# A bidirectional linear-attention scan: block-diagonal products as 64x64 quarters, state and operator products as column halves

## The chip, the cores and the metric

The kernel runs on one core of one Trainium2 chip. The metric is the device time of one execution in microseconds (us); three timed runs of the kernel before gave 1756.57, 1759.63 and 1762.25 us.

## The reference, cut to what matters

One layer of a hybrid backbone over 128 context and 2048 latent tokens, width 1024. One input projection feeds two groups of channels: 512 channels of gated short convolution, and 512 channels (8 heads of 64) of RWKV-7 mixing, which is the part that the change touches. It is run once in each direction of time, and the two outputs are added:

```python
def step(S, inp):
    r_t, w_t, k_t, v_t, kk_t, a_t = inp
    s_kk = jnp.einsum('bdhij,bdhj->bdhi', S, kk_t)
    S = (S * w_t[..., None, :] - s_kk[..., :, None] * (kk_t * a_t)[..., None, :]
         + v_t[..., :, None] * k_t[..., None, :])
    return S, jnp.einsum('bdhij,bdhj->bdhi', S, r_t)

s_final, ys = lax.scan(step, s0.astype(f32), xs)      # d = 2 directions, h = 8 heads, S is 64 x 64
ys = jnp.moveaxis(ys, 0, 2)
y = ys[:, 0] + jnp.flip(ys[:, 1], axis=1)
```

The latent scans start from cached states, the context scans from zero; then come a group norm, a bonus term, gates, and one output projection with a residual and a final norm. All inputs and outputs are float32.

## The kernel before, in words

The program has three parts on one time axis. `phase1` (to about 1000 us) makes the projections and writes the scan's operands to DRAM. `phase2` is the scan (about 1000 to 1590 us), and `phase3` the output projection, which overlaps its end.

The scan works on chunks of 64 tokens. A *unit* is one chunk of one pair of heads in one direction. A *stage* holds 16 units: eight of direction 0 (group 0) and eight of direction 1 (group 1) of the same head pair, walking towards each other; there are 17 stages (16 of latent tokens, one of context). In each stage:

- `partL` loads the operands of the chunks into `rr`: five 64-column blocks for each unit on 128 partitions, the two heads of the pair one above the other (head 0 on partitions 0 to 63, head 1 on 64 to 127).
- `partM` makes products inside a chunk. `product` multiplies one operand with two others for each unit: F (one half-step of four units at a time, `F(0)` and `F(1)`) and G, which goes to `GA`. Since the two heads must not mix, `make_bd` first copies the left operand into a 128x128 block-diagonal tile `bd` (two copies on ACT for each of two operands and each group, line 779 is the copy helper), and each unit is one 128x128 product with half of it zero. DVE masks each four units out of PSUM (lines 893). `transposes` makes Q, `blocks` sends diagonal blocks of G to DRAM.
- `partI` inverts small triangular blocks on GpSimd (lines 926 to 934), `partU` and `partW` put them together (`psU`, `psW`: 32x32 products; `zb` is the result, again block-diagonal for two heads).
- `partB` multiplies `zb` with F (`psX`, one 128x128 product for each unit), copies the result on ACT into the stacked operands `stl` and `str`, and makes from these the operator E of each unit and head (`psE`, 128x128, lines 1029 and 1030).
- `partS` is the recurrence: for eight units in turn, in both groups, `psS` = E times the stacked state and values `sv` (two heads, each 128x128 by 128x64, line 1054); DVE scales the first 64 rows into the next unit's `sv` (line 1067); the other 64 rows are the output, which `finish` takes on (`psT` is its transpose).

Stages are pipelined: while the recurrence of stage s runs, `partB` and `partU` of stage s+1 and `partM` of stage s+3 (`LA = 3`) are emitted between its steps. `MORD` says which pieces of `partM` form one emitted step, and `ORDER` between which steps the other parts go. What the engines then see is an order that the framework's scheduler makes from this with a timeline of its own, so an instruction may move ahead of or behind others. PSUM is held in small pools: two buffers for `psF`, `psG`, `psQ` (`O.pm`), two for `psX`, `psE`, `psU`, `psW`, `psT` (`O.p2`), four for `psS`.

Of the kernel before, what the change touches and what calls it, by code (L numbers as in the profile page):

```python
# [681 lines left out]
MORD = ("Ff", "GgD", "", "Q")  # L682
# [8 lines left out]
def phase2(K):  # L691
# [8 lines left out]
    def setup_first():  # L700
# [20 lines left out]
        B.bd = ring(O.r1, 2, [128, 8, 128], "bd", zero)  # L721
        B.rr = ring(O.r1, 2, [128, 5, 8, 64], "rr", presetR)
# [12 lines left out]
    def setup_rest():  # L735
# [21 lines left out]
        B.zb = O.l1.tile([128, 2, 8, 128], F32, name="zb")  # L757
# [113 lines left out]
    def partM(s, st):  # L871

        at = S["at"][s]
        for gi, g in enumerate(st.g):
            d = g.d
            rr = g.rr
# [5 lines left out]
            def transposes():  # L882
                pq = O.pm.tile([128, 4, 128], F32, tag="m", name=f"psQ{s}_{gi}")
                for k in range(4):
                    T.transpose(pq[:, k, :], rr[:, 4, 2 * k:2 * k + 2, :].rearrange("p u t -> p (u t)"), B.idt[:])
                copy("q", g.Q, pq[:])

            def product(h, dst, w, x, mask, nm):
                ps = O.pm.tile([128, 4, 128], F32, tag="m", name=f"ps{nm}{s}_{gi}_{h}")
                for i in range(4):  # L890
                    u = h * 4 + i
                    T.matmul(ps[:, i, :].rearrange("p (a b) -> p a b", b=64), w[:, u, :], x[:, :, u, :], start=True, stop=True)  # L892
                V.tensor_tensor(dst[:, h * 4:h * 4 + 4, :], ps[:], mask.unsqueeze(1).broadcast_to((128, 4, 128)), ALU.mult)  # L893

            def blocks():
# [5 lines left out]
            F = lambda h: product(h, g.F, pb, rr[:, 2:4], B.msk[:, MF[d]], "F")  # L901
            GA = lambda h: product(h, g.GA, qb, rr[:, 1::-1], B.mkg[:, MG[d]], "G")
            ops = dict(Q=transposes, F=lambda: F(0), f=lambda: F(1), G=lambda: GA(0), g=lambda: GA(1), D=blocks)
            for piece in MORD:
                for c in piece:
                    ops[c]()
                yield
# [47 lines left out]
    def partW(s, st):  # L955
# [5 lines left out]
        for n in range(2):  # L961
            for g in st.g:
# [18 lines left out]
    def partU(s, st):  # L981
# [7 lines left out]
        rows = [(slice(sl * 64, sl * 64 + 32), slice(sl * 64 + 32, sl * 64 + 64)) for sl in range(2)]  # L989
        for u in range(16):  # L990
            for r0, r1 in rows:
                T.matmul(pu[r1, u, :], st.g[u // 8].GA[r0, u % 8, 96:128], st.zr[r0, u, :], start=True, stop=True)
        for r0, r1 in rows:
# [3 lines left out]
        for u in range(16):  # L997
            for r0, r1 in rows:
                T.matmul(pw[r0, u, :], B.bu[r1, u, :], st.zc[r1, u, :], start=True, stop=True)
        zf = B.zb[:].rearrange("p d u c -> p (d u) c")  # L1000
        for r0, r1 in rows:
# [9 lines left out]
    def partB(s, st):  # L1011
        for n in range(2):
            for gi, g in enumerate(st.g):
                us = half(g, n)
                g.E.append(tl([128, 4, 2, 128], "E", 4))
                px = O.p2.tile([128, 4, 128], F32, tag="s", name=f"psX{s}_{gi}_{n}")
                for i in range(4):
                    T.matmul(px[:, i, :], B.zb[:, gi, us.start + i, :], g.F[:, us.start + i, :], start=True, stop=True)  # L1018
# [395 lines left out]
```

## Time and profile before

| | |
|---|---|
| timed runs, median (lowest, highest) | 1759.63 us (1756.57, 1762.25) |
| profiled execution, first to last instruction | 1752.9 us |
| mean granted TensorE clock | 0.972 |
| busy TensorE / weight loads / VectorE / ScalarE / GpSimd | 1647.9 / 1558.8 / 1093.0 / 870.1 / 582.1 us |
| DMA | 335.69 MB, mean 192 GB/s |

The profiled execution has no time of its own beside its span; the timed runs lie 6.7 us above it. PE is TensorE's matmuls, PEld its weight loads, DVE VectorE, ACT ScalarE, POOL GpSimd, SP the DMA-issuing SyncE. A group line gives: line of the kernel, engine, operation, tiles written <- read, shapes, count | busy us, mean ns of one | idle time of the engine just before, and what ended it. For matmuls, `128*128` is the part of the array that is used, rows by columns. Spans of matmuls overlap, so the mean ns of one is not what one costs; that is read from start to start in the order of time. Rows of stretches give for each engine the busy us and, in brackets, the number of instructions, then the granted TensorE clock (PEclk), the share of time that DMA engines were busy, and GB/s.

### The profile page before, as it was taken

The page shows a single profiled execution, that of the slowest core. Times are in us where ns is not written, and L with a number is a line of the kernel's source. Part 1 is how long each engine was busy: PE and PEld are TensorE (multiplying, and loading weights), DVE is VectorE, ACT ScalarE, POOL GpSimd, SP SyncE. Part 2 cuts the span into 40 slices and gives each one's busy share as a digit, 9 for nine tenths or more (in the row PEclk, how much of TensorE's full clock was granted, in tenths as well). Part 3 has the DMA queues.
Part 4 walks back from the last instruction along what each step waited for, and adds up shares of the span by engine and source line. Part 5 has one row for each costly group of instructions (what it writes and reads, how often), then busy time and mean ns, then how long its engine had stood idle before and what let it go on. Part 6 is the DMA issues. An engine that isn't in the chain of part 4 may idle for free. (4 is left out here: it accounts for less than half of the span.)

```text
span 1752.9 us, 33041 instructions
## 1 busy us (share of the span) xinstructions
PE 1647.9 (94%) x12400; PEld 1558.8 (89%) x12400; DVE 1093.0 (62%) x2092; ACT 870.1 (50%) x1719; POOL 582.1 (33%) x1089
## 2 busy tenths in 40 slices
PE   5999899998999999999998989999999999899998
PEld 2889898998999998999998979899999999787886
DVE  5875788866567766567764544475776666656333
ACT  4534455534143433334442367687788787633222
POOL 0011111111011101011120587777777778223221
PEclk9899999999999999999999998899999999999999
DMA  9797778785557646477666585587677875746442
GB/s 367 208 234 220 233 241 246 232 255 151 148 160 227 169 147 174 135 258 217 195 214 225 173 196 135 141 192 187 174 198 189 191 185 120 180 151 206 151 144 90
DMA packets 315825, 335.69 MB, mean 192 GB/s; under 512 B 166985, under 2 KB 263881, under 8 KB 301585
## 3 DMA queue, kind: packets, MB, share of 16 engines
q1 hardware_dynamic: 243360, 324.52, 62.6%
q10 hardware_dynamic: 70944, 4.60, 2.9%
q0 software_dynamic: 1360, 4.46, 0.7%
q8 instruction: 98, 1.61, 0.4%
q14 instruction: 63, 0.51, 0.1%
HBM read 221.42 MB, written 112.08 MB: 190 GB/s over the span
## 5 line engine op out<-in xcount | busy, mean ns | idle before, releaser
L934 POOL TENSOR_TENSOR zt<-zt,ztmp 128x30 f32<-128x30 f32 (+7 forms) x510 | 197.3, 387 | 39.3
L1054 PE MATMUL psS<-sv,E 128*128 128x64 f32 x1088 | 155.1, 277 | 1.0 <-DVE sv L1067 0.6
L1029 PE MATMUL psE<-str,stl 128*128 128x128 f32 x1088 | 144.1, 281 | 11.3 <-DVE E L1030 7.0
L1054 PEld LDWEIGHTS psS<-sv,E 128*128 128x128 f32 x1088 | 145.4, 200 | 3.3 <-DVE sv L1067 0.8
L1029 PEld LDWEIGHTS psE<-str,stl 128*128 128x128 f32 x1088 | 131.8, 194 | 14.1 <-DVE E L1030 7.9
L931 POOL TENSOR_TENSOR ztmp<-ab,zt 128x60 f32<-128x60 f32 (+7 forms) x255 | 130.8, 513 | 19.2
L1067 DVE TENSOR_TENSOR sv<-psS,pc 64x128 f32<-64x128 f32 x254 | 69.2, 277 | 92.9 <-PE psS L1054 92.2
L779 ACT COPY bd<-rr 64x512 f32<-64x512 f32 x136 | 84.0, 617 | 75.7 <-DMA rr<-scr_ops 23.3
L323 POOL TENSOR_TENSOR shk<-rawl 128x384 f32<-128x384 f32 (+1 forms) x24 | 20.7, 861 | 291.9 <-ACT rawl L319 291.9
L1030 DVE TENSOR_TENSOR E<-psE,msk 128x512 f32<-128x512 f32 x136 | 92.7, 684 | 33.0 <-PE psE L1029 32.3
L892 PE MATMUL psF<-rr,bd 128*128 128x128 f32 x544 | 80.0, 295 | 16.2 <-ACT Q L779 9.8
L892 PEld LDWEIGHTS psF<-rr,bd 128*128 128x128 f32 x544 | 70.7, 203 | 20.4 <-ACT Q L779 12.9
L1350 POOL TENSOR_TENSOR z<-z,x 128x512 f32<-128x512 f32 x32 | 43.6, 1364 | 126.6 <-DVE z L1346 105.9
L1018 PE MATMUL psX<-F,zb 128*128 128x128 f32 x544 | 78.2, 297 | 3.2 <-ACT zb L777 2.3
L197 POOL TENSOR_TENSOR hslb<-kd,hshb 128x384 fp32r<-128x384 f32 (+1 forms) x24 | 26.7, 1113 | 164.0 <-ACT hshb L196 143.5
L160 PE MATMUL mmc<-h,w 128*128 128x384 f32 (+1 forms) x192 | 67.9, 354 | 13.4 <-ACT q1r L321 9.8
L323 POOL TENSOR_TENSOR shv<-rawl 128x384 f32<-128x384 f32 (+1 forms) x24 | 25.4, 1060 | 153.4 <-ACT rawl L319 153.4
L892 PE MATMUL psG<-rr,bd 128*128 128x128 f32 x544 | 72.0, 280 | 4.4 <-DVE F L893 4.4
L1018 PEld LDWEIGHTS psX<-F,zb 128*128 128x128 f32 x544 | 71.6, 209 | 4.0 <-POOL zt L934 1.9
L892 PEld LDWEIGHTS psG<-rr,bd 128*128 128x128 f32 x544 | 65.7, 193 | 5.0 <-DVE F L893 4.8
L161 PE MATMUL mmc<-h,w 128*128 128x384 f32 (+1 forms) x192 | 66.1, 344 | 0.0
L162 PE MATMUL mmc<-h,w 128*128 128x384 f32 (+1 forms) x192 | 65.7, 342 | 0.0
(307 smaller groups left out, 5205.4 us busy)
## 6 DMA issues: line engine op xcount, KB each, us to landing
w<-scr_wsp SPq DMA_DIRECT2D x68, 1024.0 KB, 7.3
scr_wsp<-w SPq DMA_DIRECT2D x34, 1024.0 KB, 6.0
rr<-scr_ops SPq DMA_DIRECT2D x64, 512.0 KB, 4.6
scr_ops<-sp SPq DMA_DIRECT2D x160, 192.0 KB, 5.2
wr<-in_win SPq DMA_DIRECT2D x34, 512.0 KB, 6.3
ab<-scr_at SPq DMA_DIRECT2D x34, 256.0 KB, 4.2
x<-in_x SPq DMA_DIRECT2D x17, 512.0 KB, 3.8
wadas<-in_wada SPq DMA_DIRECT2D x8, 1024.0 KB, 13.0
```

Of the source, the lines that this page charges most:

```text
L160: T.matmul(ps[:, :n], w[:, 0, k], hh[:, 0, k, :n], start=k == 0, stop=False)
L161: T.matmul(ps[:, :n], w[:, 0, k], hh[:, 1, k, :n], start=False, stop=False)
L162: T.matmul(ps[:, :n], w[:, 1, k], hh[:, 0, k, :n], start=False, stop=k == 7)
L779: (V.tensor_copy if k in ON_DVE else P.copy)(dst, src)
L892: T.matmul(ps[:, i, :].rearrange("p (a b) -> p a b", b=64), w[:, u, :], x[:, :, u, :], start=True, stop=True)
L931: G.tensor_tensor(tv, ab[:, j:j + 2, j + 2:32].unsqueeze(1).broadcast_to((128, kn, 2, n)), zt[:, :kn, j:j + 2].unsqueeze(3).broadcast_to(( ...
L934: G.tensor_tensor(zt[:, :kn, j + 2:32], zt[:, :kn, j + 2:32], tv[:, :, r], ALU.subtract)
L1018: T.matmul(px[:, i, :], B.zb[:, gi, us.start + i, :], g.F[:, us.start + i, :], start=True, stop=True)
L1029: T.matmul(pe[:, i, hd, :].rearrange("p (b t) -> p b t", b=2), g.lt[:, :, hd, us.start + k + i].rearrange("p b t -> p (b t)"), g.rt[:, :, ...
L1030: V.tensor_tensor(g.E[n][:, k:k + 2].rearrange("p a b c -> p (a b) c"), pe[:].rearrange("p a b c -> p (a b) c"), B.msk[:, ME[g.d]].unsquee ...
L1054: T.matmul(sp[gi][:, q, hd, :], g.E[n][:, k, hd, :], sv[:, u, hd, :], start=True, stop=True)
L1067: r = V.tensor_tensor(dst, sp[gi][0:64, q], B.pc[0:64, d, 2 * p:2 * p + 2, c:c + 1].broadcast_to((64, 2, 64)), ALU.mult)
```

## The change

The block-diagonal operands go. F, G and X are made as 64x64 quarters of the array: one for each head, with the other head's zero block left out, and the two groups put a head's result into different halves of the partitions (`place`), so that head 0 and 1 of group 0 and of group 1 use the four quadrants. `product` and `psX` now loop over both groups inside the unit loop and hold a PSUM buffer for each group. `zb` shrinks to 64 columns. E and S are made as two column halves: each 128x128 product becomes two with 128 rows and 64 columns of the array. `rr` gets a third buffer, `bd` goes. `MORD` and the number of `partM` steps between the recurrence's steps follow.

```diff
-MORD = ("Ff", "GgD", "", "Q")
+MORD = ("F", "f", "G", "gD", "Q", "q")
...
-        B.bd = ring(O.r1, 2, [128, 8, 128], "bd", zero)
-        B.rr = ring(O.r1, 2, [128, 5, 8, 64], "rr", presetR)
+        B.rr = ring(O.r1, 3, [128, 5, 8, 64], "rr", presetR)
...
-        B.zb = O.l1.tile([128, 2, 8, 128], F32, name="zb")
+        B.zb = O.l1.tile([128, 2, 8, 64], F32, name="zb")
...
-    def make_bd(t_, src):
-        copy("b", t_[0:64, :, 64:128], src[0:64])
-        copy("c", t_[64:128, :, 0:64], src[64:128])
+    def place(g, hd):
+
+        return 1 - hd if g.d == 0 else hd
+
+    def rows(i):
+        return slice(i * 64, i * 64 + 64)
...
-            pb, qb = B.bd(), B.bd()
-            make_bd(pb, rr[:, 0])
-            make_bd(qb, rr[:, 4])
...
-            def product(h, dst, w, x, mask, nm):
-                ps = O.pm.tile([128, 4, 128], F32, tag="m", name=f"ps{nm}{s}_{gi}_{h}")
-                for i in range(4):
-                    u = h * 4 + i
-                    T.matmul(ps[:, i, :].rearrange("p (a b) -> p a b", b=64), w[:, u, :], x[:, :, u, :], start=True, stop=True)
-                V.tensor_tensor(dst[:, h * 4:h * 4 + 4, :], ps[:], mask.unsqueeze(1).broadcast_to((128, 4, 128)), ALU.mult)
+        def product(h, w, xs, dst, mask, nm):
+            ps = [O.pm.tile([128, 4, 128], F32, tag="m", name=f"ps{nm}{s}_{gi}_{h}") for gi in range(2)]
+            for i in range(4):
+                u = h * 4 + i
+                for g, p_ in zip(st.g, ps):
+                    for hd in range(2):
+                        r = rows(hd)
+                        T.matmul(p_[rows(place(g, hd)), i, :].rearrange("p (a b) -> p a b", b=64), g.rr[r, w, u, :], g.rr[r, xs, u, :], start=True, stop=True)
+            for g, p_ in zip(st.g, ps):
+                V.tensor_tensor(dst(g)[:, h * 4:h * 4 + 4, :], p_[:], mask(g).unsqueeze(1).broadcast_to((128, 4, 128)), ALU.mult)
...
-                    r = slice(64 - i * 64, 128 - i * 64)
-                    copy("g", g.gs[64:128, 1, i, us], g.GA[r, us, 0:64])
+                    copy("g", g.gs[64:128, 1, i, us], g.GA[rows(place(g, i)), us, 0:64])
...
-            for r in (r0, r1):
-                copy("z", zf[r, :, r], st.zc[r])
-            copy("n", zf[r0, :, r1], pw[r0], True)
+            for i, r in enumerate((r0, r1)):
+                copy("z", zf[r, :, i * 32:i * 32 + 32], st.zc[r])
+            copy("n", zf[r0, :, 32:64], pw[r0], True)
...
+            px = [O.p2.tile([128, 4, 128], F32, tag="s", name=f"psX{s}_{gi}_{n}") for gi in range(2)]
+            for i in range(4):
+                for gi, g in enumerate(st.g):
+                    u = half(g, n).start + i
+                    for hd in range(2):
+                        r = rows(place(g, hd))
+                        T.matmul(px[gi][rows(1 - hd), i, :], B.zb[r, gi, u, :], g.F[r, u, :], start=True, stop=True)
...
-                px = O.p2.tile([128, 4, 128], F32, tag="s", name=f"psX{s}_{gi}_{n}")
-                for i in range(4):
-                    T.matmul(px[:, i, :], B.zb[:, gi, us.start + i, :], g.F[:, us.start + i, :], start=True, stop=True)
...
-                            T.matmul(pe[:, i, hd, :].rearrange("p (b t) -> p b t", b=2), g.lt[:, :, hd, us.start + k + i].rearrange("p b t -> p (b t)"), g.rt[:, :, hd, us.start + k + i], start=True, stop=True)
+                            for b, c in enumerate((H0, H1)):
+                                T.matmul(pe[c, i, hd, :].rearrange("p (b t) -> p b t", b=2), g.lt[:, b, hd, us.start + k + i], g.rt[:, :, hd, us.start + k + i], start=True, stop=True)
...
-                    T.matmul(sp[gi][:, q, hd, :], g.E[n][:, k, hd, :], sv[:, u, hd, :], start=True, stop=True)
+                    for m_ in (H0, H1):
+                        T.matmul(sp[gi][m_, q, hd, :], g.E[n][:, k, hd, m_], sv[:, u, hd, :], start=True, stop=True)
...
-                for _ in range((2, 2, 2, 1, 1, 0, 0, 0)[i]):
+                for _ in range((1, 1, 1, 1, 1, 1, 0, 0)[i]):
```

Where the scheduler then puts the instructions of TensorE is shown in the prediction, at the places of which it speaks. Of a name such as `psE_1_01` there, the first digit is the group and the next the half-step (of E, also the half of the half-step); the letter is the product, and the number after `x` counts equal products in a row.

More of the change, by code (lines that the diff above doesn't have):

```diff
@@ new lines, in F, with GA, transposes @@
+        def F(h):
+            product(h, 0, slice(2, 4), lambda g: g.F, lambda g: B.msk[:, MF[g.d]], "F")
+        def GA(h):
+            product(h, 4, slice(1, None, -1), lambda g: g.GA, lambda g: B.mkg[:, MG[g.d]], "G")
+        def transposes(gi):
+            g = st.g[gi]
+            pq = O.pm.tile([128, 4, 128], F32, tag="m", name=f"psQ{s}_{gi}")
+            for k in range(4):
+                T.transpose(pq[:, k, :], g.rr[:, 4, 2 * k:2 * k + 2, :].rearrange("p u t -> p (u t)"), B.idt[:])
+            copy("q", g.Q, pq[:])
@@ L896, in blocks @@
+        def blocks():
+            for gi, g in enumerate(st.g):
                 dg = tl([128, 8, 32], "dg", 1, O.rI)
@@ L899, in blocks @@
                 nc.scalar.dma_start(at[gi * 8:gi * 8 + 8].rearrange("u s b j i -> (s b j) u i"), dg[:])
[L901 to L907, printed above, removed]
+        ops = dict(Q=lambda: transposes(0), q=lambda: transposes(1), F=lambda: F(0), f=lambda: F(1), G=lambda: GA(0), g=lambda: GA(1), D=blocks)
+        for piece in MORD:
+            for c in piece:
+                ops[c]()
+            yield
     def partI(s, st):
@@ L1015, in partB @@
                 g.E.append(tl([128, 4, 2, 128], "E", 4))
[L1016 to L1018 removed]
                 for hd in range(2):
[L1020 removed]
+                    copy("x" if hd else "y", g.fs[64:128, :, hd, us], px[gi][rows(1 - hd)].rearrange("p u (b t) -> p b u t", b=2), True)
             yield
```

20 lines of the change are left out of this document (6 added, 14 removed).

## The prediction

> **What bounds the kernel now.** I read the page first (its busy times and its groups), then the stretches of the scan, then the order of time on TensorE inside one stage, and last the waits. The page's first part and the groups that the change touches:
>
> ```profile
> PE 1647.9 (94%) x12400; PEld 1558.8 (89%) x12400; DVE 1093.0 (62%) x2092; ACT 870.1 (50%) x1719; POOL 582.1 (33%) x1089
> ...
> L1054 PE MATMUL psS<-sv,E 128*128 128x64 f32 x1088 | 155.1, 277 | 1.0 <-DVE sv L1067 0.6
> L1029 PE MATMUL psE<-str,stl 128*128 128x128 f32 x1088 | 144.1, 281 | 11.3 <-DVE E L1030 7.0
> ...
> L1067 DVE TENSOR_TENSOR sv<-psS,pc 64x128 f32<-64x128 f32 x254 | 69.2, 277 | 92.9 <-PE psS L1054 92.2
> L779 ACT COPY bd<-rr 64x512 f32<-64x512 f32 x136 | 84.0, 617 | 75.7 <-DMA rr<-scr_ops 23.3
> ...
> L1030 DVE TENSOR_TENSOR E<-psE,msk 128x512 f32<-128x512 f32 x136 | 92.7, 684 | 33.0 <-PE psE L1029 32.3
> L892 PE MATMUL psF<-rr,bd 128*128 128x128 f32 x544 | 80.0, 295 | 16.2 <-ACT Q L779 9.8
> ...
> L1018 PE MATMUL psX<-F,zb 128*128 128x128 f32 x544 | 78.2, 297 | 3.2 <-ACT zb L777 2.3
> ...
> L892 PE MATMUL psG<-rr,bd 128*128 128x128 f32 x544 | 72.0, 280 | 4.4 <-DVE F L893 4.4
> ```
>
> TensorE is busy 94% of the span. Each float32 product of the program stands in the trace as two passes (544 state products, x1088), each with a weight load of its own, and 128*128 is the part of the array, rows by columns, that a pass uses. A busy share alone does not say that an engine is the bound, so next the scan, first its fifteen stages from the first to the last and then seven steady ones:
>
> ```profile
> core 0: us, PE busy (x) PEld busy (x) DVE busy (x) ACT busy (x) POOL busy (x), PEclk, DMA share, GB/s
> 1021.30:1493.90 472.60, 453.13 (x5354) 440.24 (x5354) 287.00 (x589) 368.98 (x706) 361.27 (x815) 0.96 0.71 172
> 1256.50:1469.20 212.70, 206.43 (x2537) 201.25 (x2536) 142.53 (x291) 172.31 (x332) 162.07 (x361) 1.00 0.77 185
> ```
>
> A steady stage takes 212.7 / 7 = 30.4 us, of which PE is busy 29.5, ACT 24.6, POOL 23.2 and DVE 20.4. PE waits under 1 us of a stage, and what it waits for there is short:
>
> ```profile
> PE psF L892 <- ACT Q L779: 3.7, 11, 0.8
> PE psE L1029 <- ACT stl L777: 1.1, 1, 1.1
> PE psE L1029 <- DVE E L1030: 1.0, 1, 1.0
> ```
>
> So the scan is bound by how fast TensorE takes passes, and the recurrence through the state is covered: sv on DVE waited 92.2 us for psS, and psS only 0.6 us for sv. The next limits are ACT and POOL, 6 to 7 us lower. That makes the price of a pass the whole question.
>
> **The price of a pass, of a small pass and of a switch.** The order of time on TensorE, at two places of a stage:
>
> ```profile
> 1240.87 0.56 PE L1054 MATMUL psS<-sv,E 128*128 128x64 f32 x4
> 1241.26 1.11 PE L1018 MATMUL psX<-F,zb 128*128 128x128 f32 x8
> 1242.21 0.33 PE L1054 MATMUL psS<-sv,E 128*128 128x64 f32 x2
> ...
> 1253.37 1.20 PE L992 MATMUL psU<-zr,GA 32*32 32x32 f32 x64
> 1254.50 1.10 PE L1054 MATMUL psS<-sv,E 128*128 128x64 f32 x8
> 1255.44 1.11 PE L892 MATMUL psF<-rr,bd 128*128 128x128 f32 x8
> 1256.48 0.24 PE L999 MATMUL psW<-zc,bu 32*32 32x32 f32 x2
> 1256.66 0.66 PE L1054 MATMUL psS<-sv,E 128*128 128x64 f32 x4
> 1257.24 1.19 PE L999 MATMUL psW<-zc,bu 32*32 32x32 f32 x62
> 1258.37 0.66 PE L1132 MATMUL psT<-idt,y 128*128 128x128 f32 x4
> ```
>
> From start to start, four S passes and eight X passes take 1242.21 - 1240.87 = 1.34 us, 0.112 us each, although S streams 64 columns and X 128: the 128-column weight load sets the S pass. The 64 passes of U, which use two different 32*32 squares in turn, take 1.13 us with the change of shape behind them, 0.018 each, so two squares work at once. What a change of shape costs: eight F passes should take 0.90 and psW starts 1.04 later, 0.14 over; four S passes between two pieces of psW take 0.58 in place of 0.45, 0.13 over; I take 0.15. U less 0.15 is 0.98 us for 32 rounds of two, 0.031 a round. Column strips of the array are seen at the start of the kernel:
>
> ```profile
> 34.33 1.06 PE L190 MATMUL psrow<-wadas,scp 128*32 128x512 f32 x8
> 34.33 0.16 PEld L190 LDWEIGHTS psrow<-wadas,scp 128*32 128x32 f32 x8 [0.24 <-issue]
> ```
>
> Eight passes, four times as wide as an X pass, on four strips: one after another they would be about 8 x 4 x 0.112 = 3.6 us, and they take 1.06, their eight weight loads 0.16. Strips load and work at the same time, each with its own moving data.
>
> **The state products S** become two 128*64 halves, both of which can load and stream together. A round then costs what a load and a stream of 64 columns cost; no row shows it, and I put it on the line between 0.031 (32 wide) and 0.112 (128 wide): 0.058. 1088 x 0.112 = 122 us becomes 1088 rounds x 0.058 = 63: **-58 us** (ends: 0, if halves loaded in turn, which psrow speaks against; -88 at U's round).
>
> **The operator products E** are 128 wide, so a round of two halves still streams as long as one pass did: 0 (0.112 against 0.112).
>
> **F, G and X** lose their zero blocks: 1632 passes, 183 us, become 3264 quarter passes. They cost half if four quarters run together, and nothing is won if two do. The source alternates both groups, so that four stand side by side; the schedule does not keep that. TensorE in a steady stage of before, from psE_0_01 to the next E pair (the first digit of a psS or psE is the group, and xN counts products):
>
> ```order
> L1029 MATMUL psE_1_01_14274<-str_10041,stl_10035 128x128 x4
> L1054 MATMUL psS_1_0_14436<-sv_13965,E_14248 128x64 x2
> L885 MATMUL psQ_0_14482<-idt_9262,rr_9282 128x128 x4
> L1018 MATMUL psX_0_1_14379<-F_9272,zb 128x128 x4
> L1054 MATMUL psS_0_0_14432<-sv_13956,E_14240 128x64 x2
> L1018 MATMUL psX_1_1_14387<-F_9275,zb 128x128 x4
> L1054 MATMUL psS_1_0_14436<-sv_13965,E_14248 128x64 x2
> L892 MATMUL psF_1_0_14503<-rr_9283,bd_9278 128x128 x4
> ```
>
> The same place of the program now:
>
> ```order
> L1041 MATMUL psE_1_01_14884<-str_10087,stl_10081 64x128 x8
> L1067 MATMUL psS_0_0_15078<-sv_14474,E_14848 64x64 x4
> L1067 MATMUL psS_1_0_15084<-sv_14483,E_14851 64x64
> L1026 MATMUL psX_0_1_15000<-F_9266,zb 64x128 x8
> L1067 MATMUL psS_1_0_15084<-sv_14483,E_14851 64x64 x3
> L887 MATMUL psF_0_1_15124<-rr_9278 64x128 x2
> L1026 MATMUL psX_1_1_15001<-F_9269,zb 64x128 x8
> L1067 MATMUL psS_0_0_15078<-sv_14474,E_14848 64x64 x4
> L1067 MATMUL psS_1_0_15084<-sv_14483,E_14851 64x64 x4
> L1041 MATMUL psE_0_10_15024<-str_10086,stl_10080 64x128 x8
> L887 MATMUL psF_1_1_15125<-rr_9279 64x128 x8
> ```
>
> The eight X quarters of one group stand together, then those of the other; so do both halves of F and the second of G. A group alone has two quadrants, so eight quarters are four rounds of two passes, 0.9 us, as four full products were. Only psG of the first half and psX of the first half alternate:
>
> ```order
> L887 MATMUL psG_0_0_15159<-rr_9278 64x128 x2
> L887 MATMUL psG_1_0_15160<-rr_9279 64x128 x2
> L887 MATMUL psG_0_0_15159<-rr_9278 64x128 x2
> L887 MATMUL psG_1_0_15160<-rr_9279 64x128 x2
> L887 MATMUL psG_0_0_15159<-rr_9278 64x128 x2
> L1041 MATMUL psE_1_11_15054<-str_10087,stl_10081 64x128 x8
> L887 MATMUL psG_1_0_15160<-rr_9279 64x128 x2
> ```
>
> Two half-steps in six cost half: 183 x 2/6 / 2 = **-30 us** (ends: -91 if TensorE reaches past eight waiting quarters to the other group's, 0 if never four).
>
> **Switches of shape.** Before, S, E, F, G, X and the transposes all used the whole array; now S and E use 128*64, F, G and X 64*64, Q and T all of it. Counted over the whole order, neighbours of different shape rise from 131 to 506, in a steady stage from 6 to about 27. 375 x 0.15 = **+56 us**. 303 of the 506 lie between 64*64 and 128*64, a pair that this trace does not show; if that pair were free, the term would be +11.
> The Trainium skill, "TensorEngine Tiling (Array Packing)", Key Properties, says that changing the tiling mode, not just the tile, drains TensorE; by it the term stays at +56, the sum at -32, and without it the sum would be -77. The trace agrees for the pairs it has (0.13 to 0.17 us).
>
> **The rest.** The 136 copies that make the block-diagonal operand leave ACT (84 us, 4.6 of its 24.6 in a stage), and two 617 ns steps between the load of rr and F. ACT is not the bound; PE's idle before psF, 16.2 us in all, is the most that could go. Against it I set new waits of DVE's 684 ns evictions, since both groups now take both buffers of the psF pool: 0 in the sum, 15 either way. What hid S's round trip (S, then DVE's sv, 277 ns) were 0.9 to 2 us of other passes between two S pairs; 0.9 to 1.8 us remain. DMA issues do not change but for a third rr buffer.
>
> **Sum.** -58 - 30 + 56 + 0 = -32 us against the profiled span of 1752.9: 1721. The timed runs have a median of 1759.63, 6.7 us over that span, which the change does not touch: **1728 us**. A steady stage would go from 30.4 to about 28.4.
>
> **The rivals.**
> *Switches between halves and quarters are free, or the queue reaches the other group's quarters:* 45 us less, or up to 60. Nothing in the trace shows it; the squares of U overtaking one another speak a little for the second. About 1683. Chance 0.16.
>
> *The clock.* The granted clock halves after a thin stretch and stays low; TensorE's order of time there, and the stretches:
>
> ```profile
> 1217.59 1.20 PE L992 MATMUL psU<-zr,GA 32*32 32x32 f32 x64
> 1218.72 1.10 PE L1054 MATMUL psS<-sv,E 128*128 128x64 f32 x8
> 1221.28 1.01 PE L892 MATMUL psF<-rr,bd 128*128 128x128 f32 x3 [1.46 <-ACT Q L779]
> ```
>
> ```profile
> 1214.40:1217.80 3.40, 3.40 (x42) 3.28 (x42) 1.86 (x5) 2.82 (x6) 2.93 (x7) 1.00 0.72 204
> 1217.80:1221.25 3.45, 2.02 (x72) 1.84 (x64) 1.25 (x4) 3.31 (x8) 2.90 (x8) 1.00 0.87 189
> 1221.25:1224.65 3.40, 3.37 (x16) 3.08 (x16) 0.00 (x0) 2.34 (x4) 2.28 (x7) 0.50 0.44 110
> 1224.65:1228.10 3.45, 3.45 (x71) 3.27 (x71) 0.39 (x2) 1.19 (x4) 0.00 (x0) 0.50 0.83 228
> 1228.10:1231.50 3.40, 3.40 (x17) 3.40 (x17) 3.17 (x5) 1.02 (x3) 2.69 (x5) 0.50 0.41 100
> ```
>
> In the second row of stretches PE works 2.02 of 3.45 us, about half of it on 32*32 squares, waits 1.46 for Q, and then runs at 0.50 for 10.25 us: 5.1 us lost. Quarters alone fill half the array and each switch is a gap, so the stretch U, S, G, W of every stage comes near that row, and a stretch of 64*64 passes may not bring the clock back. At one such loss in each of 17 stages, 87 us; the scan now loses (1 - 0.96) x 472.6 = 19: 1728 + 68 = 1796, slower. It decides from about seven losses more than now, (32 + 5.3) / 5.1. Against it: U and W lie behind S and G as before, and the wait for Q should go, since other passes now stand between Q and F. Chance 0.24.
> The Trainium skill, "TensorE: Matmul & The Clock Gate", HAM oscillation, tells of the same halving by windows of about 3.4 us; the rows agree.
>
> *Quarters of one group wait for each other*, because both write one PSUM buffer: a group alone then costs twice, an alternating pair what it did: 183 x (4/6 x 2 + 2/6) = 305 us in place of 153: 1880. U's two squares write one buffer and overlap. Chance 0.03.
> The Trainium skill, "TensorEngine Tiling (Array Packing)", Gotcha 1, forbids different row tiles the same bank at the same time; U's 0.018 us a pass disagrees.
>
> *PE's gain turns into waits* for DVE, ACT and the operator chain, 2 us a stage: about 1757, no change. PE waits under 1 us a stage now, but its order is fixed and the fill between S pairs is shorter. Chance 0.14.
>
> **How the numbers follow.** 0.43 for the forecast, 1728, with 15 us of waits either way. The range goes from the free switches (1683) to the clock (1796); outside lie 0.03 above and tails of both rivals, near 0.15. 0.3%, 5.3 us, is about what a measurement can tell from no change. Faster: 0.43 + 0.16 + 0.02 of the waits = 0.61; same 0.09; slower 0.24 + 0.03 + 0.03 = 0.30.
>
> **What would show it.** After: psS passes x2176 at about 0.03 us each from start to start; a psE piece of four products still 0.9 us; a psX piece of one group (eight quarters) 0.9 us, an alternating one 0.45; 0.15 us over at each change of shape; steady stages of 28 to 29 us at clock 1.00 and no more losses of clock than now. Steady stages under 26 us would say that switches are free; a mean clock under 0.93 in the scan, that the gate took it; PE idle of 2 us a stage, the waits.

## The result, and the profile after

The kernel after the change took 1838.52 us (median; 1837.4 to 1840.77) against 1760.94 us of the kernel before on the same chip: 1.0435 times as long, 95% interval 1.0411 to 1.0459. 1728 us were forecast, with a range of 1683 to 1796: the sign was wrong, and the time lies outside. The profiled execution spans 1837.3 us. Its page, TensorE's busy time and the groups that answer to those of before:

```profile
PE 1634.4 (89%) x16208; PEld 1488.4 (81%) x16208; DVE 1087.9 (59%) x2093; ACT 776.9 (42%) x1583; POOL 585.7 (32%) x1087
...
L1041 PE MATMUL psE<-str,stl 128*64 128x128 f32 x2176 | 169.8, 309 | 43.2 <-ACT stl L776 25.4
...
L887 PE MATMUL psF<-rr 64*64 64x128 f32 x1088 | 89.3, 312 | 60.1 <-DMA rr<-scr_ops 18.6
...
L1067 PE MATMUL psS<-sv,E 128*64 128x64 f32 x2176 | 112.6, 233 | 15.6 <-DVE sv L1080 15.4
...
L1026 PE MATMUL psX<-F,zb 64*64 64x128 f32 x1088 | 65.3, 281 | 5.2 <-ACT zb L776 3.2
```

Idle time of TensorE has moved in before psE (11.3 us before, 43.2 now) and psF (16.2, now 60.1). The fifteen stages of the scan that took 472.60 us with PE busy for 453.13:

```profile
core 0: us, PE busy (x) PEld busy (x) DVE busy (x) ACT busy (x) POOL busy (x), PEclk, DMA share, GB/s
1043.20:1567.20 524.00, 435.29 (x8615) 375.79 (x8613) 277.82 (x588) 290.66 (x593) 354.72 (x792) 0.88 0.60 150
```

PE works 18 us less, the stretch lasts 51 us longer, and the granted clock falls from 0.96 to 0.88. What TensorE waited for in the scan (waiting group, releaser, us in total, times, longest):

```profile
PE psE L1041 <- ACT stl L776: 25.4, 6, 10.5
PE psF L887 <- issue: 17.5, 2, 11.6
PE psS L1067 <- DVE sv L1080: 15.4, 11, 3.5
PE psF L887 <- DMA rr<-scr_ops: 13.3, 3, 10.4
PE psF L887 <- ACT Q L778: 12.7, 5, 3.9
PE psE L1041 <- ACT str L776: 10.5, 6, 4.5
```

No single wait stands out; they are few and long (up to 11.6 us), where in the ten stages of the table below the kernel before has none over 1.5 us. One of them in the order of time, on POOL, SP and PE:

```profile
1151.40 0.60 POOL L943 DMA_DIRECT2D scr_zt<-zt  x1 [0.30 <-POOL zt L942]
...
1153.90 1.32 SPq L985 DMA_DIRECT2D zc<-scr_zt  x2
1155.32 1.19 SPq L870 DMA_DIRECT2D rr<-scr_ops  x2
...
1158.68 1.21 SPq L922 DMA_DIRECT2D ab<-scr_at  x2
...
1160.22 0.69 PE L887 MATMUL psF<-rr 64*64 64x128 f32 x4 [10.41 <-DMA rr<-scr_ops]
```

SP issues its loads in order. It stands before zc until POOL's store of zt has landed; the load of rr, for which TensorE waits 10.41 us, and the next input of POOL, ab, come only behind it.

To compare kernels I took the ten stages from the first psS of stage 4 to that of stage 14 and split them by the trace's records: time in which no matmul or weight load is under way (waits), busy time, and what of the busy time fell into spells of halved clock. Half of the last is lost to the clock; busy time less that half is the work at full clock. All in us a stage:

| kernel (ratios with their intervals below) | time ratio | stage | waits | work at full clock | lost to the clock |
|---|---|---|---|---|---|
| before | 1 | 31.0 | 0.9 | 29.3 | 0.9 |
| after | 1.0435 | 35.7 | 5.8 | 27.2 | 2.7 |
| halves only (e2) | 1.0054 | 31.5 | 1.9 | 28.8 | 0.9 |
| quarters only (e3) | 1.0542 | 38.3 | 5.9 | 29.8 | 2.6 |
| groups apart (e7) | 1.0246 | 33.9 | 3.7 | 28.7 | 1.5 |
| rr and dg doubled (e12) | 1.0321 | 34.2 | 5.8 | 26.6 | 1.8 |
| + ab on ACT (e15) | 1.0163 | 31.5 | 3.3 | 26.8 | 1.4 |
| + G first (e16) | 0.9974 | 29.8 | 2.2 | 26.4 | 1.2 |
| before, short recursion (e10) | 0.9890 | 29.8 | 0.6 | 29.2 | 0 |
| e12, short recursion (e13) | 0.9953 | 30.4 | 2.4 | 26.6 | 1.5 |
| e7, short recursion (e14) | 0.9927 | 29.7 | 0.9 | 28.9 | 0 |

TensorE's work fell by 2.1 us a stage, 36 us over 17 stages, where 32 were forecast. Waits (+4.9) and halved clock (+1.8) took it back three times over. The question is where the waits come from.

Of the 84 us by which the profiled execution grew, 63 lie between the first psS and the last. The first psS comes 19 us later, at 1053.4 in place of 1034.2, and 11 of these stand ahead of the first psF, before the scan has begun. With the ring of two of e6, the changed kernel has its first psF at 941.6, earlier than before's 943.2, so these 11 us are not shown to be the change's.

Microseconds that a run gained or lost are below always its median less that of the kernel before on the same chip: the kernel after stands at +78.

### The profile page after: what moved, and what is told of

Its sections match the earlier page's. It is cut to its first block, busy times and chain, and to the rows that moved or that the text cites. A ratio compares the mean times of both kernels' runs of the same rounds, so it can differ in the third digit from the quotient of the medians.

```text
span 1837.3 us, 40674 instructions
## 1 busy us (share of the span) xinstructions
PE 1634.4 (89%) x16208; PEld 1488.4 (81%) x16208; DVE 1087.9 (59%) x2093; ACT 776.9 (42%) x1583; POOL 585.7 (32%) x1087
## 5 line engine op out<-in xcount | busy, mean ns | idle before, releaser
L1041 PE MATMUL psE<-str,stl 128*64 128x128 f32 x2176 | 169.8, 309 | 43.2 <-ACT stl L776 25.4
L1041 PEld LDWEIGHTS psE<-str,stl 128*64 128x64 f32 x2176 | 141.0, 157 | 59.9 <-ACT stl L776 27.2
L887 PE MATMUL psF<-rr 64*64 64x128 f32 x1088 | 89.3, 312 | 60.1 <-DMA rr<-scr_ops 18.6
L1067 PE MATMUL psS<-sv,E 128*64 128x64 f32 x2176 | 112.6, 233 | 15.6 <-DVE sv L1080 15.4
L1067 PEld LDWEIGHTS psS<-sv,E 128*64 128x64 f32 x2176 | 92.3, 142 | 37.8 <-DVE sv L1080 19.1
L887 PEld LDWEIGHTS psF<-rr 64*64 64x64 f32 x1088 | 62.7, 150 | 73.3 <-issue 23.5
L323 POOL TENSOR_TENSOR shk<-rawl 128x384 f32<-128x384 f32 (+1 forms) x24 | 20.8, 866 | 292.6 <-ACT rawl L319 292.6
L160 PE MATMUL mmc<-h,w 128*128 128x384 f32 (+1 forms) x192 | 69.5, 362 | 13.5 <-ACT q1r L321 10.3
L1026 PE MATMUL psX<-F,zb 64*64 64x128 f32 x1088 | 65.3, 281 | 5.2 <-ACT zb L776 3.2
L889 DVE TENSOR_TENSOR F<-psF,msk 128x512 f32<-128x512 f32 x68 | 45.9, 684 | 40.0 <-PE psF L887 26.1
L161 PE MATMUL mmc<-h,w 128*128 128x384 f32 (+1 forms) x192 | 68.0, 354 | 0.0
L162 PE MATMUL mmc<-h,w 128*128 128x384 f32 (+1 forms) x192 | 67.7, 353 | 0.0
L160 PE MATMUL mmgb<-h,w 128*128 128x384 f32 (+1 forms) x192 | 65.2, 340 | 0.0
L162 PE MATMUL mmgb<-h,w 128*128 128x384 f32 (+1 forms) x192 | 64.9, 338 | 0.0
L161 PE MATMUL mmgb<-h,w 128*128 128x384 f32 (+1 forms) x192 | 64.7, 337 | 0.0
```

The lines of the kernel that those rows point to most:

```text
L160: T.matmul(ps[:, :n], w[:, 0, k], hh[:, 0, k, :n], start=k == 0, stop=False)
L161: T.matmul(ps[:, :n], w[:, 0, k], hh[:, 1, k, :n], start=False, stop=False)
L162: T.matmul(ps[:, :n], w[:, 1, k], hh[:, 0, k, :n], start=False, stop=k == 7)
L887: T.matmul(p_[rows(place(g, hd)), i, :].rearrange("p (a b) -> p a b", b=64), g.rr[r, w, u, :], g.rr[r, xs, u, :], start=True, stop=True)
L1026: T.matmul(px[gi][rows(1 - hd), i, :], B.zb[r, gi, u, :], g.F[r, u, :], start=True, stop=True)
L1041: T.matmul(pe[c, i, hd, :].rearrange("p (b t) -> p b t", b=2), g.lt[:, b, hd, us.start + k + i], g.rt[:, :, hd, us.start + k + i], start=T ...
```

## The experiments

### Which part of the change

**e1: G before F.** `MORD = ("G", "gD", "F", "f", "Q", "q")` in the kernel after.

> The changed kernel with one line other: MORD = ("G", "gD", "F", "f", "Q", "q"), so that G and the blocks for GpSimd come at steps 0 and 1 of the recurrence, not 2 and 3. Theory A (the loop load rr - F, G - blocks - GpSimd's inversion - zc, closed through SyncE's queue, is what became late): below 1790 us, PE's waits in the scan half of the changed kernel's 130 us or less, SyncE's wait for GpSimd's store back from 106 to some 50 us, clock 0.95 or more. Theory B (the many changes of shape and the thin use of the array bring the clock down by themselves): 1825 to 1850 us, clock 0.93, since 483 of 506 changes of shape stay.

1819.88 us, ratio 1.0353 (1.0328 to 1.0378). SP's wait for zt left the head of its list, and TensorE waited for rr itself: 64.5 us in nine waits before psG. The wait moved, and a fifth of the loss went.

**e2: halves only.** The kernel before, with S and E alone cut in column halves:

```diff
-                    T.matmul(sp[gi][:, q, hd, :], g.E[n][:, k, hd, :], sv[:, u, hd, :], ...)
+                    for m_ in (H0, H1):
+                        T.matmul(sp[gi][m_, q, hd, :], g.E[n][:, k, hd, m_], sv[:, u, hd, :], ...)
```

> The kernel before with the column halves of S and E alone; F, G, X and the order of the pieces stay as before. 443 changes of shape (before 131, changed kernel 506). Theory A: 1735 to 1765 us, as S saves 58 us and 312 changes of shape cost 47. Theory B: above 1810 us, clock below 0.94.

1765.44 us, ratio 1.0054 (1.0037 to 1.0072): +9. It has 443 changes of shape where before has 131, and no more halved clock than before: here changes of shape by themselves neither cost the loss nor bring the clock down. The halves won nothing all the same: TensorE's work fell by 0.5 us a stage, and its waits rose by 1.0.

**e3: quarters only.** The kernel after with S and E as whole products again.

> The changed kernel with S and E as whole 128x128 products again; F, G, X as quarters, pieces in the changed order. 453 changes of shape. Theory A: slow as the changed kernel or nearly, 1800 to 1850 us, SyncE's wait for GpSimd's store above 80 us. Theory B: 1810 to 1850 us as well; if the halves were the fault, 1750.

1852.47 us, ratio 1.0542 (1.0526 to 1.0558): +96. The loss belongs to the quarters part, which still holds the new order of pieces and both groups taken at once; e7 parts these.

**e4: blocks late.** `MORD = ("Ff", "Gg", "Q", "D")` in the kernel before.

> The kernel before with MORD = ("Ff", "Gg", "Q", "D"): the blocks for GpSimd leave one step of the recurrence later for group 0 (step 1 in place of 0) and two later for group 1 (step 4 in place of 2); no product changes, 131 changes of shape. Theory A: slower, 1780 to 1830 us, with waits on zc and ab as in the changed kernel. Theory B: 1755 to 1770 us, clock 0.97.

1755.27 us, ratio 0.9983 (0.9962 to 1.0005): nothing. In its trace the scheduler stored dg about where it did before, so this run tells little.

### The rr buffers, and the order of the groups

**e5: two rr buffers for each group** (four halves, each pair around one identity block), in place of a ring of three:

```diff
-        B.rr = ring(O.r1, 3, [128, 5, 8, 64], "rr", presetR)
+        B.rr = ring(O.r1, 2, [128, 9, 8, 64], "rr", presetR)
...
-            g.rr = B.rr()
+            g.rr = B.rr() if gi == 0 else st.g[0].rr
+            g.at = (0, 1, None, 3, 2) if gi == 0 else (7, 8, None, 5, 6)
```

> The change with two rr buffers for each group (four halves in two pair tiles that share the identity block; group 0 loads in one more small transfer a stage) in place of three in a ring; `yo` is written over `sg` to make room. Theory C (one group's rr buffer comes free only with the last piece of the stage, so its next load is issued in time for nothing and stands in SP's queue behind others): TensorE's waits for rr go (below 10 us in the stretch of the scan, from some 36), the waits of SP for zt fall, and the time falls to 1740-1785 us. Rival (the quarters themselves are at fault: changes of shape, or the PSUM buffers of both groups taken together): rr is no longer waited for, and the time stays at 1810-1840 us, with the waits at psE and psS.

1832.74 us, ratio 1.0443 (1.0378 to 1.0507). The waits for rr are gone from TensorE's list, as expected, and the time did not move: they came back as 54.5 us before psE for str.

**e6: a ring of two.**

> The change with an rr ring of two in place of three: both groups' next loads must wait for this stage's last piece. Theory C: a larger dose of the same harm, waits for rr of 100 us and more on TensorE in the scan and 1870-1950 us. Rival (buffers don't matter, the quarters are at fault): within 15 us of the change as it is, 1825-1850 us.

1825.92 us, ratio 1.0414 (1.0341 to 1.0487). The larger dose did no harm. Theory C, that the rr buffers are the cause, falls in this form.

**e7: groups apart.** F, G and Q of group 0, then of group 1, as before; still quarters:

```diff
-MORD = ("F", "f", "G", "gD", "Q", "q")
+MORD = ("Ff", "GgD", "", "Q")
...
-            ps = [O.pm.tile(..., name=f"ps{nm}{s}_{gi}_{h}") for gi in range(2)]
+            gi = cur[0]
+            g = st.g[gi]
+            p_ = O.pm.tile(..., name=f"ps{nm}{s}_{gi}_{h}")
```

> The change with F, G and the transposes done for one group after the other as in the kernel before (its order of pieces, a ring of two), still as 64x64 quarters, X still for both groups, S and E in halves. Theory C (what was lost is the time between a group's last use of rr and its next need): near the kernel before and the run with halves alone, 1750-1780 us, waits for rr under 15 us. Rival (quarters and the changes of shape that they bring are at fault, whatever their order): over 1810 us.

1797.5 us, ratio 1.0246 (1.0176 to 1.0315): +42, between both expectations. Its longest waits are before psE for str. One of them, on SP, ACT and PE:

```profile
1208.48 1.34 SPq L990 DMA_DIRECT2D zc<-scr_zt  x2
...
1211.56 1.28 SPq L848 DMA_DIRECT2D stl<-scr_ops  x2
...
1218.06 0.40 ACTq L912 DMA_DIRECT2D scr_at<-dg  x1
1218.56 1.21 ACT L776 ACTIVATE str<-psX 64x512 f32<-64x512 f32 x2 [8.08 <-DMA stl<-scr_ops]
...
1219.82 1.98 PE L1046 MATMUL psE<-str,stl 128*64 128x128 f32 x16 [7.24 <-ACT str L776]
```

dg was ready at 1209.8, yet ACT issued its store at 1218.06 and stood still until then. The records name the same completion semaphore for that store and for the second load of stl, which SP could issue only behind zc, at 1212.25. Of ACT's 8.08 us, 5.8 are the time from that load's issue to its landing, and the rest its late issue behind zc. So here a late load of SP's stops ACT, and through it TensorE and dg's store, which POOL needs next.

### POOL's loop

Here is what the prediction took for 23.2 us a stage. POOL in the kernel before, from the clearing of zt to the next stage:

```profile
1260.75 0.52 POOL L919 MEMSET zt<- 128x512 f32 x1 [4.46 <-DMA scr_zt<-zt]
...
1261.97 0.20 POOL L923 COPY dgp<-ab 128x16 f32<-128x16 f32 x1 [0.36 <-DMA ab<-scr_at]
...
1288.27 0.62 POOL L935 DMA_DIRECT2D scr_zt<-zt  x1 [0.30 <-POOL zt L934]
...
1291.82 0.20 POOL L923 COPY dgp<-ab 128x16 f32<-128x16 f32 x1 [2.94 <-DMA ab<-scr_at]
```

From its first instruction on ab to the store of zt lie 26.3 us, and the next stage begins 3.55 us later: 29.85 in all. (Of the 3.55, 2.94 are a wait for ab, so this row does not yet show POOL as the limit; e10 and e16 do.) ACT's, POOL's and SP's waits in the kernel before:

```profile
ACT dg L897 <- DMA scr_at<-dg: 1.3, 1, 1.3
```

```profile
POOL dgp L923 <- DMA ab<-scr_at: 33.3, 12, 7.6
```

```profile
SPq L978 <- DMA scr_zt<-zt: 45.6, 12, 9.2
```

The same in the kernel after:

```profile
ACT dg L907 <- DMA scr_at<-dg: 42.3, 16, 5.7
```

```profile
POOL dgp L931 <- DMA ab<-scr_at: 76.8, 10, 12.8
```

```profile
SPq L985 <- DMA scr_zt<-zt: 106.3, 14, 14.7
```

All three have grown. The two groups' dg used to be stored some 12 us apart in a stage of 30; now they follow one another in one buffer.

**e8: two buffers for `dg`.** `tl([128, 8, 32], "dg", 2, O.rI)`.

> The change with two buffers for `dg` in place of one: in the trace of the change ACT sits 42 us in the scan, 16 times, before the second group's dg until the first group's store of dg has landed (5.7 us at most), with the copies of str, stl, Q and zb queued behind it; before, the two groups' dg lay half a stage apart and no such wait shows. Theory D (this wait is what was lost): 1770-1795 us, and TensorE's waits in the scan fall by half. Theory P (the floor is POOL's chain, some 26.5 us from its first to its last instruction and 3 us to the next stage's first, and the waits come from it): the wait goes to another place, 1815-1840 us.

1811.51 us, ratio 1.0355 (1.0322 to 1.0389): +61, so 16 us are gained and the rest stays.

**e9: short recursion**, `for m in range(8)` in place of `range(15)` in the kernel after. It leaves out seven of the fifteen steps of the inversion, so zt is only part of the inverse and the outputs are not the layer's; this and the other runs with the short recursion only show times.

> The change with POOL's recursion cut from 15 steps to 8 (zt is then only part of the inverse): about 12 us less of POOL a stage, nothing else touched. Theory P: POOL's chain no longer sets a floor of 29.6 us a stage, SP no longer waits for zt, and the time falls to 1700-1745 us. Theory D (ACT's wait for the store of dg): that wait is untouched, and the time stays at 1800-1830 us.

1802.5 us, ratio 1.0303 (1.0269 to 1.0336): +52, 25 us gained.

**e10: the control**, the same cut in the kernel before.

> The control: the kernel before with the same cut of POOL's recursion from 15 steps to 8. Theory P and theory D both: TensorE sets the stages of before (29.3 us of work and 0.9 of waits in each), so it gains little, 1740-1757 us. If it falls below 1735 us, POOL's chain set the kernel before as well.

1731.36 us, ratio 0.989 (0.9852 to 0.9928). The cut takes 19 us off before as well, so the 25 of e9 are little more than the control: POOL's length alone is not what the change lost, and the kernel before stood against it too. Its stage fell from 31.0 to 29.8 us; 0.9 of these 1.2 us are halved clock, of which none is left, and 0.3 are waits.

**e11: both**, e8 with the short recursion.

> The change with two buffers for `dg` and POOL's recursion cut to 8 steps. If both waits were the loss, the stage falls to TensorE's own work of 27 us and a little more, some 3 us a stage under before: 1690-1725 us. If neither was (the quarters' changes of shape and the PSUM buffers taken in pairs are at fault), it stays over 1800 us.

1790.51 us, ratio 1.024 (1.0205 to 1.0274), near the rival's 1800. But the trace shows a wait that was small in the kernel after. Stage end in e11, on PE and SP:

```profile
1195.86 1.09 PE L901 MATMUL psQ<-idt,rr 128*128 128x128 f32 x8
...
1196.67 4.57 SPq L1118 DMA_DIRECT2D sg<-scr_sg  x1
...
1203.94 0.48 SPq L922 DMA_DIRECT2D ab<-scr_at  x1
...
1206.89 0.38 SPq L870 DMA_DIRECT2D rr<-scr_ops  x1
...
1211.46 1.12 PE L887 MATMUL psF<-rr 64*64 64x128 f32 x8 [9.35 <-DMA rr<-scr_ops]
```

psQ is done with the buffer at 1197, psF of the other group wants a filled one at 1202, and SP, after 4.57 us at the issue of sg and a wait of 2.7 before ab, loads it behind ab at 1206.89. TensorE waited for rr 59.9 us in all, in 11 waits, against 13.3 in the kernel after. With dg and POOL out of the way, rr binds after all: the waits hide one another.

### Taking the waits away together

**e12: e5 and e8 together** (`so` gets one buffer to make room).

> The change with two rr buffers for each group (as in the run with four halves) and two buffers for `dg` together. Alone, the first left the time where it was and the second took 20 us off; with `dg` and POOL's chain both relieved TensorE still sat 60 us before psF for rr, so each wait may hide the next. Theory W (several waits stand one behind the other: rr, dg, POOL's chain): 1775-1800 us, TensorE's waits for rr gone, ACT's wait for the store of dg gone, what is left stands at zc. Rival (taking both groups at once is at fault by itself, through PSUM and changes of shape): 1805-1830 us.

1812.18 us, ratio 1.0321 (1.0287 to 1.0356): +60, on the rival's side. No wait for rr and none for dg's store is left, but SP waits for zt longer than in the kernel after (106.3). The wait, and one such place on ACT, POOL and SP:

```profile
SPq L988 <- DMA scr_zt<-zt: 137.8, 13, 21.3
```

```profile
1213.52 1.00 ACTq L912 DMA_DIRECT2D scr_at<-dg  x2
1221.70 0.60 POOL L946 DMA_DIRECT2D scr_zt<-zt  x1 [0.30 <-POOL zt L945]
...
1224.19 0.61 SPq L988 DMA_DIRECT2D zc<-scr_zt  x1
...
1225.66 1.62 SPq L925 DMA_DIRECT2D ab<-scr_at  x2
...
1231.18 0.20 POOL L934 COPY dgp<-ab 128x16 f32<-128x16 f32 x1 [6.22 <-DMA ab<-scr_at]
```

dg's stores are issued by 1214.5, but SP stands before zc and issues ab at 1225.66, so POOL starts at 1231.18, 9.5 us after its last store. This is a closed loop: POOL, zt, SP, ab, POOL. In the kernel before, ab of the next stage stood ahead of zc on SP in all eleven stages from 4 to 14; in the kernel after zc is ahead in five of the eleven.

**e13: e12 with the short recursion.**

> The last kernel with POOL's recursion cut to 8 of 15 steps as well: all three waits relieved. Theory W: TensorE's own work is left, 27 us and 1 to 2 us of waits a stage against 29.8 of the control (before with the short recursion, 0.989 of before): 1690-1720 us, a ratio of 0.965 to 0.98. Rival (both groups at once, or the changes of shape, are at fault): 1770 us and more.

1744.03 us, ratio 0.9953 (0.9919 to 0.9986): -9. From e12 the cut takes 68 us, where it took 19 from before and 25 from the kernel after. And against e11, from which it differs by the rr buffers (and the tiles that made room for them), it is 49 us less, where the same buffers alone gave 1 us in e5. The waits do stand one behind the other, but the forecast of 1690 to 1720 was missed: 2.4 us of waits and 1.5 of clock a stage are left.

**e14: e7 with the short recursion.**

> The run with F, G and the transposes by group (quarters, X for both groups) with POOL's recursion cut to 8 steps. There ACT's store of dg lay up to 8 us behind loads that SP could issue only after zt, and TensorE waited for str. Theory W (with the groups apart neither rr nor dg binds, POOL's chain alone is left): 1715-1745 us, at or under the control. Rival (the quarters cost this by themselves): 1770-1790 us, the 41 us above before less the 19 that the control gained.

1739.75 us, ratio 0.9927 (0.9899 to 0.9955): -13, 6 us over the control. With the groups apart, quarters and halves cost next to nothing when POOL is out of the way.

**e15: ab on ACT's queue**, in e12, POOL's work whole:

```diff
-            D(ab[h * 64:h * 64 + 64].rearrange("p j i -> p (j i)"), ...)
+            nc.scalar.dma_start(ab[h * 64:h * 64 + 64].rearrange("p j i -> p (j i)"), ...)
```

> The kernel with two rr buffers for each group and two for `dg`, with the loads of ab issued by ACT instead of SP; POOL's recursion whole. In that kernel's trace SP issues zc of one stage ahead of ab of the next in about half of the stages; there ab waits behind SP's 11 us for zt though dg's store has long landed, POOL stands idle for some 10 us with the chain POOL, zt, SP, ab, POOL closed, and these stages take 39 to 41 us. Theory O (this order of SP's is the largest loss; POOL's chain alone, overlapped, takes 29.6 us a stage): 1740-1770 us, no stage over 35 us. Rival (POOL's chain is too long whatever the order, or both groups at once are at fault): 1795-1815 us.

1783.02 us, ratio 1.0163 (1.0123 to 1.0204): +29. The queue alone gives 31 us, but not the 1770 expected.

**e16: e15 with G first**, `MORD = ("G", "gD", "F", "f", "Q", "q")`.

> The same with G and the blocks first and F after them: dg's store leaves POOL's next input ready some 8 us earlier in the stage. Theory O: within 10 us of the last kernel, 1735-1770 us, since POOL's chain then sets the stage. If what counts is how late ab comes, it is 15 us and more faster than the last kernel.

1748.76 us, ratio 0.9974 (0.9951 to 0.9997): -5. That is 34 us more, so how early ab comes does count, as the second expectation had it. Of the changed kernels that do all of the work this is the fastest; it is level with before, with an interval that ends at 0.9997. Its scan is shorter: 536.6 us from the first psS to the last in the profiled execution, against 554.4, but its first psS comes 10 us later. ACT's load of ab, and POOL behind it:

```profile
1178.15 0.52 ACTq L925 DMA_DIRECT2D ab<-scr_at  x1
```

```profile
1186.01 0.60 POOL L946 DMA_DIRECT2D scr_zt<-zt  x1 [0.30 <-POOL zt L945]
1188.41 0.52 POOL L930 MEMSET zt<- 128x512 f32 x1 [1.79 <-DMA scr_zt<-zt]
...
1189.33 0.21 POOL L934 COPY dgp<-ab 128x16 f32<-128x16 f32 x1
...
1216.29 0.62 POOL L946 DMA_DIRECT2D scr_zt<-zt  x1 [0.30 <-POOL zt L945]
1218.83 0.52 POOL L930 MEMSET zt<- 128x512 f32 x1 [1.92 <-DMA scr_zt<-zt]
...
1219.76 0.20 POOL L934 COPY dgp<-ab 128x16 f32<-128x16 f32 x1
```

ab is asked for 11 us before POOL takes it, and POOL waits for nothing but its own store (1.8 and 1.9 us here). Even so its stage takes 1219.76 - 1189.33 = 30.4 us, and the eleven periods from stage 4 on take 29.6 to 31.3, with no wait for ab over 0.1. So POOL sets the stage of this program. (TensorE's ten stages in the table average 29.8, since the last of them, near the end of the scan, takes 24.7; the other nine average 30.4.)

**e17: ab on ACT's queue in e7** (groups apart).

> The run with F, G and the transposes by group (1797 us), with the loads of ab issued by ACT. There 4 of 11 stages have zc ahead of ab on SP, and they are the ones of 37 to 40 us. Theory O: 1745-1770 us. Rival (quarters cost 41 us by themselves): 1785-1800 us.

1801.96 us, ratio 1.027 (1.0228 to 1.0311): no gain. Theory O falls for this kernel, though its ten stages did get shorter, 32.8 us against 33.9 in e7: in the profiled executions the four stages before them took 135 us in place of 125.

**e18: the control**, ab on ACT's queue in the kernel before.

> The control: the kernel before with the loads of ab issued by ACT. In before ab stands ahead of zc in every steady stage, so theory O expects no gain: 1745-1762 us. If it gains 15 us and more, the queue held before back too, and the gains of the other runs must be read against it.

1768.74 us, ratio 1.0084 (1.0054 to 1.0115). The move gains nothing there and costs some 15 us, so the 31 us of e15 were not something that any kernel gets.

## Why the prediction was wrong

**The price of passes, halves, quarters and switches: right.** TensorE in a stage of the kernel after:

```profile
1197.40 0.51 PE L1067 MATMUL psS<-sv,E 128*64 128x64 f32 x10
1197.84 0.44 PE L887 MATMUL psF<-rr 64*64 64x128 f32 x6
1198.21 1.09 PE L1041 MATMUL psE<-str,stl 128*64 128x128 f32 x16
1199.14 0.40 PE L1067 MATMUL psS<-sv,E 128*64 128x64 f32 x8
1199.47 0.32 PE L887 MATMUL psF<-rr 64*64 64x128 f32 x1
1199.47 0.32 PE L1026 MATMUL psX<-F,zb 64*64 64x128 f32 x1
...
1200.19 0.33 PE L887 MATMUL psF<-rr 64*64 64x128 f32 x2
1200.28 0.28 PE L1026 MATMUL psX<-F,zb 64*64 64x128 f32 x2
```

The E piece takes 0.93 us from start to start (0.9 forecast). Eight S halves with the change of shape behind them take 0.33, where four rounds at 0.058 and 0.15 make 0.38. The piece of one group's eight X quarters (16 passes) with a change behind it takes 1.02 in most places of the scan (0.9 and 0.15 forecast). By the same prices the halves alone should give -58 + (443 - 131) x 0.15 = -11 us, 0.7 a stage, and e2's work fell by 0.5; the quarters alone -30 + (453 - 131) x 0.15 = +18 us, 1.1 a stage, and e3's work rose by 0.5; the whole change -32, and the work fell by 36. The forecast held eight quarters of one group that stand alone to two at a time. In part they do better, since quarters of other products join them: two psF passes start at 1200.19, between two pairs of psX whose starts lie 0.11 us apart (1200.17 and 1200.28).

**"The next limits are ACT and POOL, 6 to 7 us lower": this step failed.** The 23.2 us were POOL's busy time. Its recursion is a chain: with the gaps between its instructions it takes 26.3 us in before and 27.0 in e16, and 3.3 to 3.5 us of storing, waiting for that store and clearing follow before the next (e16), so POOL's stage is about 30 us, as long as TensorE's 30.4, where the prediction had 7 us of room. e16, where POOL never waits for its input, stops at 30.4, and e10 shows that the kernel before gains as soon as this chain is shorter. So some 0.6 us a stage (31.0 less 30.4) was to be had, even with every wait gone.
The Trainium skill, "Perfetto Trace Analysis", Identifying the Most-Contended Engine, says to use the occupancy percentage of GPSIMD to find the bottleneck engine. The measurement decides against it here: POOL was 76% busy (162.07 of 212.70 us), and its chain, its store and the clearing fill some 30 of the 30.4 us.

**"0 in the sum, 15 either way" for new waits, "DMA issues do not change but for a third rr buffer": this failed too.** 15 us over the scan were allowed; the waits rose by 4.9 us a stage. With POOL's loop as long as the stage, what delays ab or zc lengthens it, and the change delays them in three ways that were in the diff or the order: both groups' dg follow each other in one buffer (e8: 16 us), one group's rr is wanted some 5 us after another's last use and loaded behind ab (e11), and zc moved ahead of ab in SP's queue (e15: 31 us). That G comes late in the stage cost the last 34 us (e16): in stages 4 to 9 the second group's dg is stored 15.5 to 17.5 us after the stage's first psS in the kernel before, 20.8 to 31.3 in the kernel after, 7.1 to 10.9 in e16. Each alone gives little since the next one takes its place: e5 1 us, e8 16, G first 14 (e1); all of them, in e16, take +78 to -5. TensorE's own saving was there in e16 (26.4 us of work a stage against 29.3), but POOL's period of 30.4 us leaves it no use.

**The rivals.** "PE's gain turns into waits" named the right thing, but priced it at 2 us a stage where it was 4.9, and looked for it on DVE, ACT and the operator chain rather than in POOL's loop and SP's queue. The clock's mark (under 0.93 in the scan) was met with 0.88; but as a cause it comes second: e2 has the changes of shape and not the loss of clock, e16 has quarters and loses 1.2 us a stage, and in the kernel after each of the twelve spells of halved clock in ten stages (two in before) begins in or just behind a wait of TensorE of 1.0 to 7.0 us.
The Trainium skill, "TensorE: Matmul & The Clock Gate", HAM oscillation, tells of a wait for a transfer that is long enough to throttle TensorE, so that the next work starts cold. The trace agrees in that the spells go with waits, but few of these waits were for a transfer. The table's sums follow only roughly: 5.8 us of waits go with 2.7 lost to the clock, 5.8 with 1.8 in e12, and 0.9 with 0.9 in before and with 0 in e14.
Free switches and quarters that wait for each other in one bank are both out, by the prices above. That taking both groups at once, with both PSUM buffers of a pool, is the fault by itself is out as well: e16 does so and stands at -5.

**What stays open.** Why e7 and e17, with the groups apart, stay at 1.025 and 1.027 while POOL's work is whole; e14 shows only that POOL's loop has to do with it. What the 2.4 us of waits a stage in e13 are, which is 1.8 more than in the control. Whether e16 would reach TensorE's own 26.4 us a stage with a shorter chain on POOL was not run. Nor was it tried to give ACT's store a semaphore of its own.

## What to carry to other kernels

Before costing a change on the busiest engine, measure the period of every engine's chain, from its first instruction in one stage to its first in the next, with its own gaps, stores and waits; an engine that is 76% busy may have no slack. Where a stage passes through an in-order queue, write down what stands ahead of what, and check every single-buffered tile whose two uses the change moves together. When a suspected wait is removed and nothing happens, look for the wait that took its place before dropping the theory: here the short recursion took 25 us off alone and 68 once two other waits were gone.

## What the hardware showed that was not expected

- 64x64 quarters of different products share a round: two psF passes start between two pairs of psX 0.11 us apart (1200.17 to 1200.28), the time that one pair takes alone. Which quadrants they use the records do not say.
- POOL waits 1.8 to 2.8 us a stage for the store that it has just issued before it clears zt for the next stage, though there are two buffers (e16, ten stages).
- A store issued by ACT waited 7.5 us (1210.48 to 1218.01) for a load issued by SP: the two carry the same completion semaphore, and ACT waits on it just ahead of the store (e7).
